# Low parts of weights on VectorE alone, splits drawn ahead and interleaved norms in a two-layer hybrid backbone

## The chip, the cores and the metric

The kernel runs on one core of a Trainium2 chip. The metric is the device time of one execution in microseconds (us). Four of the core's engines matter: TensorE (PE in the rows; PEld is its weight load), VectorE (DVE), ScalarE (ACT) and GpSimd (POOL). SyncE (SP) issues most DMA transfers. Every engine works through its own queue in order.

## What is computed

Two layers, an even one (Fourier mixing and a Hyena convolution) and an odd one (gated linear attention, GLA, and HGRN2), each with a feed-forward network (FFN) before and behind the mixer. There are 256 latent tokens and 256 context tokens, that is four tiles of 128 tokens; the context goes through the same weights with its own modulation. All is fp32. The part that this change touches is the FFN and its closing:

```python
def _modulate(x, shift, scale):
    return (_ln(x) * (1.0 + scale) + shift).astype(x.dtype)

def _post_ln(x, y, g, b):
    z = ALPHA * x.astype(jnp.float32) + y.astype(jnp.float32)
    return (_ln(z) * g + b).astype(x.dtype)

def _ffn_sublayer(x, shift, scale, gate, w_in, w_out, g, b):
    a, u = jnp.split(_modulate(x, shift, scale) @ w_in, 2, axis=-1)
    y = (jax.nn.silu(a) * u) @ w_out
    return _post_ln(x, 0.5 * gate * y, g, b)
```

D_MODEL is 1024 and D_FF is 2816, 22 blocks of 128. The modulation vectors (shift, scale, gate) are products of SiLU(c) and SiLU(c_ctx) with a weight of [1024, 9216] for each layer.

## The kernel before

**Weights.** An fp32 product is made of three products of a faster type: every weight unit `raw` [128, 1024] (512 KB, loaded on SP's queue into one of three buffers) is split into a high part `hi`, a cast on ACT (line 78), and a low part `lo = raw - hi` (line 79), on DVE or on POOL as the unit's flag `pool` says. Per block PE multiplies hi by hi, hi by lo and lo by hi (lines 463 to 465). `Stream.split_to(i)` emits the splits of all units up to i; `ahead_load` and `ahead_split` set how far loads and splits run ahead of use. Most split parts go into their own buffers (whi, wlo); units with the flag `spare` go into general buffers (S, names hi and lo).

**FFN, first product.** `ffn()` begins with a head of four units (`tm_head`), token tile by token tile; a head can only begin when the norm of its tile is there. Then 20 loops f = 2..21 have two units each (`pa` and `pu`, 24 matmuls of 512 columns each); behind them ACT makes SiLU(pa), DVE the product `sa` (line 617), and ACT and POOL split it into `hh` (lines 226 and 227). Between them `step(n)` advances background generators (`bg`) by n: mainly the modulation products, where each step multiplies one half of a weight block by both conditions, two DVE instructions `mt` (line 243), and, in one of the FFNs, the spectrum of the next mixer (tiles pr, eb).

**FFN, second product.** `ffn_close()` runs 22 units k over tiles 0 and 1 (pass 1, 12 matmuls for each k), then the same units over tiles 2 and 3 (pass 2). In pass 2 the last TAIL = 6 units run tile by tile: first tile 2, then tile 3, 36 matmuls each. `closing()` of a tile is post_ln (z, statistics st and mv, x), `norm` (mv, rstd, nb) and `to_hT`, the transposes that the next head needs. The closings of tiles 0 and 1 alternate in the background of pass 2; `done(t)` is called when a tile is ready, `fill(k)` behind each unit. Three FFNs of four tiles are closed thus, with keys c00, c01 and c10; the last FFN has two tiles and its own code.

**What sets the order.** The program is unrolled, and each engine takes its instructions in the order in which the Python code emits them; `bg`, `step`, `flush` and the table G, read through `g_(key, default)`, set it. The table's keys of the form c00l31 choose DVE (0) or POOL (1) for the low part of hT of a tile (here 3) and half (here 1).

Of the kernel before, what the change touches and what calls it, by code (L numbers as in the profile page):

```python
# [38 lines left out]
class Stream:  # L39
# [26 lines left out]
    def split_to(self, i):  # L66
        while self.n_split <= min(i, len(self.units) - 1):
# [3 lines left out]
            if split:  # L71
                w = self.raw.pop(j)
                if spare:
                    hi, lo = self.spare([P, 1024], F32R, "hi"), self.spare([P, 1024], F32R, "lo")
                else:
                    hi = self.pool.tile([P, 1024], F32R, tag="whi", name=f"whi{j}")
                    lo = self.pool.tile([P, 1024], F32R, tag="wlo", name=f"wlo{j}")
                self.nc.scalar.copy(hi, w)  # L78
                (self.nc.gpsimd if pool else self.nc.vector).tensor_tensor(lo, w, hi.bitcast(F32), op=ALU.subtract)  # L79
                self.split[j] = (hi, lo)  # L80
            self.n_split += 1

# [13 lines left out]


G0 = {"qlh33": 1, "qlh41": 1, "qlh43": 1, "of11": 2, "m0e00": 1, "qot12": 1, "m0l10": 0, "c10s2": 3, "c00S3": 2, "c10l30": 0, "m1w1": 1, "qot01": 0, "of": 2, "c10l31": 0, "o3": 4, "qoo0": 0, "m0l30": 0, "qeo6": 1, "c00l11": 0, "c00d2": 5, "qot23": 0, "ex21": 1, "es000": 1, "qei9": 1, "m0k": 0, "m0v2": 1, "fp3": 0, "ec010": 0, "ez3": 0, "fp1": 0, "qei3": 1, "m0l00": 0, "m0l01": 0, "qeo4": 0, "qeh2": 0, "ec012": 0, "es013": 0, "ec113": 0, "ec002": 1, "ec112": 0, "m0w0": 0, "m0v3": 1, "ec000": 1, "qei10": 1, "m0w1": 1, "m0a": -2, "m0v1": 1, "es003": 1, "m0w3": 1, "qei0": 0, "m0v0": 1, "m0l11": 1, "qeh0": 1, "es102": 1, "es012": 0, "qei2": 0, "m0e01": 1, "ez0": 1, "m0e10": 1, "qeh3": 1, "es100": 0, "m0e11": 1, "ex23": 1, "m0w2": 0, "es001": 1, "m0t3": 5, "c10w3": 1, "m0t2": 3, "qoi6": 1, "q00o14": 1, "o2": 1, "c00s2": 2, "qot02": 1, "m0d3": 2, "o1": 2, "m0s0": 2, "c01l01": 1, "of10": 1, "c00t3": 0, "c10w0": 0, "qoi16": 1, "c01l00": 1, "m0S1": 3, "m1w0": 1, "c00t1": 3, "qoi9": 1, "ex13": 1, "qoo6": 0, "m1l00": 1, "m1e11": 1, "of02": 3, "qoo7": 1, "c01d3": 3, "qoi14": 0, "m0t0": 2, "m1k": 6, "m1l10": 0, "qoi10": 0, "qoo5": 0, "of13": 3, "m0S2": 2, "m1e10": 0, "ec003": 0, "c10l10": 1, "qei8": 0, "of03": 4, "c00S2": 2, "qot20": 0, "c10e00": 0, "c00d3": 4, "m1a": 4, "of01": 3, "qot03": 0, "m0A": 2, "c01t3": 2, "q10o12": 1, "ec100": 0, "q01h0": 1, "qoi7": 0, "c10w1": 1, "qoi13": 0, "qot11": 0, "c00l10": 0, "m0s3": 2, "c00t2": 0, "c00l31": 1, "of12": 3, "c01d0": 3, "m1t0": 3, "qei4": 1, "qot32": 1, "c00F": 1, "c01S2": 2, "m1e01": 0, "qot00": 1, "m1l11": 0, "m1e00": 1, "c01v2": 1, "ok1": 2, "qlh02": 0, "c01l10": 0, "qoi15": 0, "SPN": 5, "qot21": 1, "q00o19": 0, "c00A": 2, "qoi11": 0, "qoi8": 1, "m1d0": 3, "c01S3": 2, "m0s1": 3, "m1d1": 5, "m1s1": 2, "ok0": 4, "of00": 1, "Fc0": 0, "Fw0": 1, "Ftl10": 1, "Ftl21": 1, "Fw2": 0, "Ftl11": 0, "Fc1": 1, "Ffl11": 0, "Fab0": 0, "Fte30": 0, "FxT11": 1, "Fs20": 0, "Ffl01": 0, "es101": 1, "qei5": 0, "m0e31": 1, "c01b2": 0, "m0e21": 0, "c10e21": 0, "qoo4": 0, "qlh00": 1, "qoo3": 0}
G = {}
SEEN = {}  # L100

# [27 lines left out]
def kernel(ctx: ExitStack, tc: tile.TileContext, a, out, stop=None):  # L129
# [450 lines left out]
    def queue_ffn(l, i):  # L580
# [4 lines left out]
                ws.add(a["ffn_in"][l, i, f, au], True, False, au == 1)  # L585
        for s in range(2):
            for k in range(KF):
                ws.add(a["ffn_out"][l, i, P * k:P * k + P, :], True, s == 1 and KF - TAIL <= k < KF - 1, g_(f"q{l}{i}o{k}", int(k % 2 == 1 and k < KF - 3)) if s and k > 11 else k % 2)

    def ffn(l, i, extra=(), head=None):  # L590
        hs = [{0: S([P, 2, 2, L], F32R, name="hh")} for s in range(2)]
# [9 lines left out]
        for f in range(2, KF):  # L601
# [9 lines left out]
                todo = None  # L611
            step(1)
            fm_unit(pu)
            step(2)
            sa = H([P, T], name="sa")
            act.activation(sa, pa, AF.Silu)
            dve.tensor_tensor(sa, sa, pu, op=ALU.mult)  # L617
# [5 lines left out]
    def ffn_close(l, i, hs, nxt):  # L623
# [9 lines left out]

        def fill(k):
            if k % 2:
                step(1)
            if k in range(10, 18, 2):
                next(loads)

        def closing(t, y, late=False):  # L640
            g, b, gates = ln
            return close(t, y, gates[t // 2], g, b, 2 * ALPHA, 4 * EPS, nxt, late, not late)

        y = tok_out(lhs, KF, (0, 1), fill)
        flush()
# [2 lines left out]
        bg.append(alternate(closing(0, y[0]), closing(1, y[1])))  # L648

        def done(t, y):  # L650
            if t == 3:
                hs.clear()
            ws.split_spare(ws.pos + g_(f"{k0}a{t}", 2 * t - 3))
            if t == 3:
                flush()
            bg.append(closing(t, y, True))
            now.append(t)

        def fill(k):
            if now:  # L660
                step(g_(f"{k0}s3", 1))
            elif k >= KF - TAIL:
                step(g_(f"{k0}s2", 1))
            else:
                if k >= KF - TAIL - 3:
                    ws.split_spare(ws.pos + g_(f"{k0}b{KF - TAIL - k}", 1))
                step(g_(f"{k0}s1", 2) if k > g_(f"{k0}s0", 2) else 1)

        now = []
        tok_out(lhs, KF, (2, 3), fill, TAIL, done)  # L670


# [55 lines left out]
    def spectrum(o, hd, w3, win, cs, skip, T=None):  # L728
# [78 lines left out]
        if early:  # L807
            for n in todo[:2]:
                pks[n] = product(*n)
                yield  # L810
        rs = scale()
        yield
# [1103 lines left out]
```

## Time and profile before

| quantity | value |
|---|---|
| median of 3 runs (lowest, highest) | 1894.14 us (1893.0, 1899.78) |
| profiled execution, time | 1893.39 us |
| its span | 1891.6 us |
| PE busy | 1761.0 us, 93% |
| DVE busy | 1259.5 us, 67% |
| ACT busy | 724.8 us, 38% |
| POOL busy | 721.6 us, 38% |

The rows of a later section are from this profiled execution. Times are counted from the start of its span. A row of a timeline gives the start, the duration, the engine, the line, the operation, what is written and read, and in brackets how long the engine had been idle before it and for what it had waited. PEclk is the granted clock of PE as a share of the full one.

### The profile page before, as it was taken

Reading aid. Unit: us, or ns where it says so; the run is one execution under the profiler, and the core shown is the slowest. Engines: PE = TensorE matmul, PEld = TensorE weight load, DVE = VectorE, ACT = ScalarE, POOL = GpSimd, SP = SyncE. Lnnn points to the kernel's source line nnn. Section 1 sums busy time; section 2 is a strip of 40 time slices with the busy share of each in tenths; the row PEclk is TensorE's granted clock in tenths of the full one; section 3 lists DMA queues with packets and bytes.
Section 4 is the critical chain, followed back from the end, with each engine's and each line's share of the span. In section 5 each row is a group of like instructions: output and inputs, shape, how many; then the busy total and the mean of one; then the engine's idle time right before and its main releaser. Section 6 shows DMA issues by size and latency. Waiting matters only on the chain. (4 is left out here: it accounts for less than half of the span.)

```text
span 1891.6 us, 22049 instructions
## 1 busy us (share of the span) xinstructions
PE 1761.0 (93%) x8236; PEld 1425.5 (75%) x8236; DVE 1259.5 (67%) x1674; ACT 724.8 (38%) x1070; POOL 721.6 (38%) x467
## 2 busy tenths in 40 slices
PE   6989999998987999999999999999988999879998
PEld 5767778876866778777887787788867778757887
DVE  6688887267599768885247688812377484676755
ACT  5422233344434342223334422323354463443443
POOL 2445434453356223333445233334454353341000
PEclk9989999999998999999999999999999999889999
DMA  8536654644313145553464455433644223335563
GB/s 317 214 132 240 227 189 166 238 167 150 112 45 123 65 164 202 208 203 130 154 233 177 150 213 199 162 110 138 232 166 145 83 91 90 134 131 201 206 215 137
DMA packets 91499, 314.91 MB, mean 166 GB/s; under 512 B 10848, under 2 KB 11584, under 8 KB 91392
## 3 DMA queue, kind: packets, MB, share of 16 engines
q1 hardware_dynamic: 85952, 297.09, 44.0%
q0 software_dynamic: 4576, 15.91, 2.6%
q8 instruction: 64, 1.05, 0.2%
q10 hardware_dynamic: 864, 0.51, 0.1%
q14 instruction: 43, 0.35, 0.1%
HBM read 308.18 MB, written 4.24 MB: 165 GB/s over the span
## 5 line engine op out<-in xcount | busy, mean ns | idle before, releaser
L79 DVE TENSOR_TENSOR wlo<-raw,whi 128x1024 fp32r<-128x1024 f32 x195 | 261.5, 1343 | 330.7 <-ACT whi L78 328.9
L79 POOL TENSOR_TENSOR wlo<-raw,whi 128x1024 fp32r<-128x1024 f32 x137 | 345.9, 2525 | 316.9 <-ACT whi L78 278.4
L78 ACT CAST whi<-raw 128x1024 fp32r<-128x1024 f32 x332 | 343.8, 1050 | 264.9 <-PE y L465 151.9
L243 DVE SCALAR_TENSOR_TENSOR mt<-mraw,cb 128x1024 bf16<-128x1024 f32 x256 | 395.8, 1599 | 11.2 <-DMA mraw<-in_mod_w_dram 8.3
L465 PE MATMUL pu<-hT,wlo 128*128 128x512 f32 x576 | 225.7, 392 | 4.7 <-DVE wlo L79 4.7
L463 PE MATMUL pu<-hT,whi 128*128 128x512 f32 x576 | 225.8, 392 | 0.0
L464 PE MATMUL pu<-hT,whi 128*128 128x512 f32 x576 | 225.4, 391 | 0.0
L227 POOL TENSOR_TENSOR hh<-sa,hh 128x256 fp32r<-128x256 f32 x120 | 87.1, 747 | 344.6 <-ACT hh L226 344.6
L465 PE MATMUL pa<-hT,wlo 128*128 128x512 f32 x480 | 191.3, 398 | 12.0 <-DVE wlo L79 12.0
L463 PE MATMUL pa<-hT,whi 128*128 128x512 f32 x480 | 191.5, 399 | 8.8 <-ACT whi L78 8.7
L464 PE MATMUL y<-wlo,hh 128*128 128x512 f32 x468 | 183.2, 391 | 6.8 <-DVE wlo L79 6.1
L464 PE MATMUL pa<-hT,whi 128*128 128x512 f32 x480 | 189.1, 394 | 0.0
L463 PE MATMUL y<-whi,hh 128*128 128x512 f32 x468 | 182.9, 391 | 0.2 <-ACT whi L78 0.2
L465 PE MATMUL y<-whi,hh 128*128 128x512 f32 x468 | 182.2, 389 | 0.0
L226 ACT CAST hh<-sa 128x256 fp32r<-128x256 f32 x120 | 42.8, 404 | 294.7 <-DVE sa L617 294.7
L465 PEld LDWEIGHTS pu<-hT,wlo 128*128 128x128 f32 x576 | 108.8, 189 | 28.3 <-DVE wlo L79 5.6
L463 PEld LDWEIGHTS pu<-hT,whi 128*128 128x128 f32 x576 | 109.0, 189 | 23.6 <-ACT hh L226 0.8
L464 PEld LDWEIGHTS pu<-hT,whi 128*128 128x128 f32 x576 | 108.9, 189 | 22.6
L465 PEld LDWEIGHTS pa<-hT,wlo 128*128 128x128 f32 x480 | 91.3, 190 | 39.7 <-DVE wlo L79 21.1
L463 PEld LDWEIGHTS pa<-hT,whi 128*128 128x128 f32 x480 | 91.4, 190 | 34.3 <-ACT whi L78 15.7
L464 PEld LDWEIGHTS y<-wlo,hh 128*128 128x128 f32 x468 | 87.8, 188 | 28.6 <-DVE wlo L79 8.4
L464 PEld LDWEIGHTS pa<-hT,whi 128*128 128x128 f32 x480 | 91.4, 190 | 18.7
(419 smaller groups left out, 3272.2 us busy)
## 6 DMA issues: line engine op xcount, KB each, us to landing
raw<-in_ffn_out_dram SPq DMA_DIRECT2D x154, 512.0 KB, 3.4
mraw<-in_mod_w_dram SPq DMA_DIRECT2D x144, 512.0 KB, 5.9
raw<-in_ffn_in_dram SPq DMA_DIRECT2D x120, 512.0 KB, 3.8
raw<-in_ffn_tm_dram SPq DMA_DIRECT2D x44, 512.0 KB, 3.3
raw<-in_od_fm_dram SPq DMA_DIRECT2D x17, 512.0 KB, 3.2
raw<-in_od_tm_dram SPq DMA_DIRECT2D x16, 512.0 KB, 3.3
raw<-in_ffn_head_dram SPq DMA_DIRECT2D x12, 512.0 KB, 4.4
raw<-in_ev_in_dram SPq DMA_DIRECT2D x12, 512.0 KB, 3.5
```

The lines of the kernel that those rows point to most:

```text
L78: self.nc.scalar.copy(hi, w)
L79: (self.nc.gpsimd if pool else self.nc.vector).tensor_tensor(lo, w, hi.bitcast(F32), op=ALU.subtract)
L226: act.copy(dst_hi, src)
L227: (lo_eng or dve).tensor_tensor(dst_lo, src, dst_hi.bitcast(F32), op=ALU.subtract)
L243: dve.scalar_tensor_tensor(H([P, D], BF16, "mt"), w, 1.0, cb[s], op0=ALU.mult, op1=ALU.mult, accum_out=acc[:, s, b:b + 1])
L463: pe.matmul(o, lhsT=wh, rhs=xh, start=start, stop=False)
L464: pe.matmul(o, lhsT=wh, rhs=xl, start=False, stop=False)
L465: pe.matmul(o, lhsT=wl, rhs=xh, start=False, stop=stop)
```

## The change

- Every low part of a weight is made on DVE; the flags `pool` no longer have an effect. 164 lows move from POOL to DVE.
- Four more low parts of hT (tile 3) go to DVE.
- In pass 2 the units k = 13 to 20 use general buffers for their split parts, before only 16 to 20; the buffers of hh are released unit by unit (`pop`) and not at the end.
- The loops of the first product take 1 and 2 background steps in turn behind `pu`, before always 2.
- In pass 2 `split_to` runs ahead by up to four units more from k = 11 on, and during tile 2's tail it splits the next head's four units. `done(2)` no longer splits; `done(3)` interleaves the closings of tiles 2 and 3 in the order 2, 3, 2, 3, 3, 2.
- A spectrum that is not early waits three empty steps before its scaling.

```diff
-                (self.nc.gpsimd if pool else self.nc.vector).tensor_tensor(lo, w, hi.bitcast(F32), op=ALU.subtract)
+                self.nc.vector.tensor_tensor(lo, w, hi.bitcast(F32), op=ALU.subtract)
...
+G0.update({f"{k}l3{g}": 0 for k in ("c00", "c01", "c10", "m0") for g in range(2)})
...
-                ws.add(a["ffn_out"][l, i, P * k:P * k + P, :], True, s == 1 and KF - TAIL <= k < KF - 1, ...
+                ws.add(a["ffn_out"][l, i, P * k:P * k + P, :], True, s == 1 and KF - TAIL - 3 <= k < KF - 1, ...
...
-            step(2)
+            step(1 + f % 2)
...
         def fill(k):
             if k % 2:
+                hs[0].pop(k // 2)
                 step(1)
...
         def done(t, y):
-            if t == 3:
+            if t == 2:
+                flush()
+                ln[2][0] = None
+                bg.append(closing(t, y, True))
+                older.append(bg[-1])
+            else:
                 hs.clear()
-            ws.split_spare(ws.pos + g_(f"{k0}a{t}", 2 * t - 3))
-            if t == 3:
-                flush()
-            bg.append(closing(t, y, True))
+                g2, g3 = older.pop(), closing(t, y, True, True)
+                for g in (g2, g3, g2, g3, g3, g2):
+                    next(g, None)
+                bg.clear()
+                bg.extend([g2, g3])
             now.append(t)
 
         def fill(k):
             if now:
-                step(g_(f"{k0}s3", 1))
+                step(1)
             elif k >= KF - TAIL:
-                step(g_(f"{k0}s2", 1))
+                step(1)
+                ws.split_to(first + min(KF + k - (KF - TAIL), KF + 3))
             else:
-                if k >= KF - TAIL - 3:
-                    ws.split_spare(ws.pos + g_(f"{k0}b{KF - TAIL - k}", 1))
+                if k % 2:
+                    hs[1].pop(k // 2)
                 step(g_(f"{k0}s1", 2) if k > g_(f"{k0}s0", 2) else 1)
+                ws.split_to(first + k + 2 + {11: 1, 12: 1, 13: 2, 14: 3, 15: 4}.get(k, 0))
...
+        else:
+            for _ in range(3):
                 yield
         rs = scale()
```

The first place is a loop of the first product of the second FFN, on DVE: wlo is the low part of a weight unit, mt a modulation product, sa the product behind the two units. Before:

```order
L79 TENSOR_TENSOR wlo_6638<-raw_6546,whi_6637 128x1024
L243 SCALAR_TENSOR_TENSOR mt_6667,acc_6530<-mraw_6612,cb_5443 128x1024
L243 SCALAR_TENSOR_TENSOR mt_6669,acc_6530<-mraw_6612,cb_5445 128x1024
L243 SCALAR_TENSOR_TENSOR mt_6703,acc_6530<-mraw_6618,cb_5443 128x1024
L243 SCALAR_TENSOR_TENSOR mt_6705,acc_6530<-mraw_6618,cb_5445 128x1024
L243 SCALAR_TENSOR_TENSOR mt_6707,acc_6530<-mraw_6665,cb_5443 128x1024
L243 SCALAR_TENSOR_TENSOR mt_6709,acc_6530<-mraw_6665,cb_5445 128x1024
L617 TENSOR_TENSOR sa_6711<-sa_6711,pu_6634 128x512
```

One low part and six mt stand between two products. The same engine and place in the changed kernel:

```order
L79 TENSOR_TENSOR wlo_6599<-raw_6507,whi_6598 128x1024
L244 SCALAR_TENSOR_TENSOR mt_6628,acc_6408<-mraw_6573,cb_5443 128x1024
L244 SCALAR_TENSOR_TENSOR mt_6630,acc_6408<-mraw_6573,cb_5445 128x1024
L79 TENSOR_TENSOR wlo_6635<-raw_6543,whi_6634 128x1024
L244 SCALAR_TENSOR_TENSOR mt_6664,acc_6408<-mraw_6579,cb_5443 128x1024
L244 SCALAR_TENSOR_TENSOR mt_6666,acc_6408<-mraw_6579,cb_5445 128x1024
L618 TENSOR_TENSOR sa_6668<-sa_6668,pu_6595 128x512
```

A second low part, from POOL, stands between the mt, and this loop has four mt; the next one has six.

The second place is the end of tile 2 in pass 2 of the first FFN, on DVE. raw86 and raw87 are the last two units of the pass, raw88 to raw91 the next head's; z is the sum at the start of tile 2's closing. Before:

```order
L79 TENSOR_TENSOR lo459_3443<-raw86_3416,hi458_3442 128x1024
L79 TENSOR_TENSOR wlo87_3455<-raw87_3428,whi87_3454 128x1024
L331 TENSOR_TENSOR z464_3494<-y414_3013,gate413_2921 128x512
L337 SCALAR_TENSOR_TENSOR z464_3494<-x30_175,z464_3494 128x512
L338 BN_STATS st465_3495<-z464_3494 128x6
```

The closing follows the pass's last low part at once. In the changed kernel:

```order
L79 TENSOR_TENSOR wlo87_3437<-raw87_3410,whi87_3436 128x1024
L79 TENSOR_TENSOR lo467_3449<-raw88_3428,hi466_3448 128x1024
L79 TENSOR_TENSOR lo469_3461<-raw89_3434,hi468_3460 128x1024
L79 TENSOR_TENSOR lo471_3473<-raw90_3446,hi470_3472 128x1024
L79 TENSOR_TENSOR lo473_3485<-raw91_3458,hi472_3484 128x1024
L332 TENSOR_TENSOR z474_3506<-y414_3013,gate413_2921 128x512
```

The four lows of the next head now stand ahead of the closing.

The third place is between the closings of tiles 2 and 3, on DVE: x, st and mv, rp and nb are the end of tile 2's, the second z is tile 3's. Before:

```order
L353 SCALAR_TENSOR_TENSOR x469_3526<-z464_3494,rstd467_3516,lnb411_2845 128x1024
L304 BN_STATS st472_3543<-x469_3526 128x6 x2
L306 BN_AGGR mv473_3546<-st472_3543 128x2
L79 TENSOR_TENSOR lo475_3551<-raw90_3464,hi474_3550 128x1024
L233 TENSOR_SCALAR rp479_3561<-mv473_3546 128x1
L395 SCALAR_TENSOR_TENSOR nb471_3542<-mv473_3546,rstd478_3560 128x1
L331 TENSOR_TENSOR z485_3582<-y416_3015,gate413_2921 128x512
```

A low part of the head stood within tile 2's norm, and tile 3 began behind it. In the changed kernel:

```order
L354 SCALAR_TENSOR_TENSOR x479_3538<-z474_3506,rstd477_3528,lnb411_2844 128x1024
L305 BN_STATS st482_3555<-x479_3538 128x6 x2
L307 BN_AGGR mv483_3558<-st482_3555 128x2
L234 TENSOR_SCALAR rp485_3561<-mv483_3558 128x1
L332 TENSOR_TENSOR z486_3564<-y416_3015,gate413_2921 128x512
L396 SCALAR_TENSOR_TENSOR nb481_3554<-mv483_3558,rstd484_3560 128x1
L338 SCALAR_TENSOR_TENSOR z486_3564<-x41_221,z486_3564 128x512
```

Tile 3's first instruction stands between rp and nb of tile 2, and the low part is gone from here.

## Rows read from the trace of the kernel before

**Rows 1.** Windows by stage: us, busy time (and instructions) by engine, PEclk, DMA share, GB/s.

```profile
95.00:319.00 224.00, 206.23 (x895) 164.62 (x894) 190.35 (x235) 58.03 (x94) 95.02 (x65) 0.96 0.53 192
319.00:381.00 62.00, 62.00 (x275) 51.33 (x274) 15.84 (x13) 26.31 (x28) 33.37 (x20) 1.00 0.66 228
381.00:441.00 60.00, 55.54 (x244) 43.62 (x243) 43.33 (x52) 29.51 (x37) 31.26 (x16) 1.00 0.51 176
480.00:648.00 168.00, 151.43 (x702) 123.68 (x701) 141.39 (x203) 67.69 (x106) 78.51 (x45) 0.95 0.26 90
687.00:916.00 229.00, 222.68 (x970) 180.25 (x969) 164.37 (x207) 65.31 (x105) 79.79 (x60) 1.00 0.51 189
1074.00:1289.00 215.00, 210.77 (x923) 171.77 (x922) 137.67 (x172) 63.09 (x100) 73.57 (x57) 1.00 0.49 177
1421.00:1459.00 38.00, 30.77 (x199) 28.32 (x197) 28.64 (x38) 19.24 (x35) 15.10 (x10) 0.91 0.37 129
```

The engines stand in the order PE, PEld, DVE, ACT, POOL.

**Rows 2.** Waits of PE over the span: waiting <- releaser: us, stops, mean us.

```profile
PE pa L465 <- DVE wlo L79: 12.0, 21, 0.6
...
PE pa L463 <- ACT whi L78: 8.7, 13, 1.7
...
PE pr L758 <- DVE eb L803: 7.6, 1, 7.6
```

**Rows 3.** The page's costliest groups: busy us, mean ns | idle before, releaser.

```profile
L79 DVE TENSOR_TENSOR wlo<-raw,whi 128x1024 fp32r<-128x1024 f32 x195 | 261.5, 1343 | 330.7 <-ACT whi L78 328.9
L79 POOL TENSOR_TENSOR wlo<-raw,whi 128x1024 fp32r<-128x1024 f32 x137 | 345.9, 2525 | 316.9 <-ACT whi L78 278.4
...
L243 DVE SCALAR_TENSOR_TENSOR mt<-mraw,cb 128x1024 bf16<-128x1024 f32 x256 | 395.8, 1599 | 11.2 <-DMA mraw<-in_mod_w_dram 8.3
L465 PE MATMUL pu<-hT,wlo 128*128 128x512 f32 x576 | 225.7, 392 | 4.7 <-DVE wlo L79 4.7
```

**Rows 4.** Timeline of a loop of the second FFN, ACT, DVE and POOL.

```profile
843.76 2.00 ACT L78 CAST whi<-raw 128x1024 fp32r<-128x1024 f32 x2
...
845.89 2.51 POOL L79 TENSOR_TENSOR wlo<-raw,whi 128x1024 fp32r<-128x1024 f32 x1 [0.82 <-POOL hh L227]
846.07 3.41 DVE L243 SCALAR_TENSOR_TENSOR mt<-mraw,cb 128x1024 bf16<-128x1024 f32 x1
849.41 1.21 DVE L243 SCALAR_TENSOR_TENSOR mt<-mraw,cb 128x1024 bf16<-128x1024 f32 x1
...
855.14 0.68 DVE L617 TENSOR_TENSOR sa<-sa,pu 128x512 f32<-128x512 f32 x1
856.34 1.43 POOL L227 TENSOR_TENSOR hh<-sa,hh 128x256 fp32r<-128x256 f32 x2 [7.94 <-ACT hh L226]
856.48 2.00 ACT L78 CAST whi<-raw 128x1024 fp32r<-128x1024 f32 x2
857.55 1.30 DVE L79 TENSOR_TENSOR wlo<-raw,whi 128x1024 fp32r<-128x1024 f32 x1 [1.73 <-ACT whi L78]
```

**Rows 5.** Timeline of DVE, closings of tiles 2 and 3 of the first FFN.

```profile
441.09 0.69 DVE L331 TENSOR_TENSOR z<-y,gate 128x512 f32<-128x512 f32 x1 [0.82 <-PE y L465]
...
449.13 3.41 DVE L353 SCALAR_TENSOR_TENSOR x<-z,rstd,lnb 128x1024 f32<-128x1024 f32 x1 [0.44 <-POOL rstd L234]
...
456.01 0.68 DVE L331 TENSOR_TENSOR z<-y,gate 128x512 f32<-128x512 f32 x1
...
468.39 0.16 DVE L395 SCALAR_TENSOR_TENSOR nb<-mv,rstd 128x1 f32<-128x1 f32 x1 [0.73 <-POOL rstd L234]
```

**Rows 6.** DMA issues in 400:450: count, KB each, median us to landing.

```profile
raw<-in_ffn_out_dram SPq DMA_DIRECT2D x11, 512.0 KB, 3.3
raw<-in_ev_tm_dram SPq DMA_DIRECT2D x4, 512.0 KB, 4.3
```

**Rows 7.** Timeline of DVE at the end of the odd mixer, two OG scalings.

```profile
1641.88 1.14 DVE L1419 SCALAR_TENSOR_TENSOR OG<-OG,rr,rg 128x128 f32<-128x128 f32 x4 [1.12 <-POOL rr L234]
...
1652.59 5.41 DVE L1419 SCALAR_TENSOR_TENSOR OG<-OG,rr,rg 128x128 f32<-128x128 f32 x4 [1.16 <-POOL rr L234]
```

More of the change, by code (lines that the diff above doesn't have):

```diff
@@ L587, in queue_ffn @@
             for k in range(KF):
-                ws.add(a["ffn_out"][l, i, P * k:P * k + P, :], True, s == 1 and KF - TAIL <= k < KF - 1, g_(f"q{l}{i}o{k}", int(k % 2 == 1 and k < KF - 3)) if s and k > 11 else k % 2)
+                ws.add(a["ffn_out"][l, i, P * k:P * k + P, :], True, s == 1 and KF - TAIL - 3 <= k < KF - 1, g_(f"q{l}{i}o{k}", int(k % 2 == 1 and k < KF - 3)) if s and k > 11 else k % 2)
     def ffn(l, i, extra=(), head=None):
@@ L638, in fill, with closing @@
                 next(loads)
-        def closing(t, y, late=False):
+        def closing(t, y, late=False, fine=False):
             g, b, gates = ln
-            return close(t, y, gates[t // 2], g, b, 2 * ALPHA, 4 * EPS, nxt, late, not late)
+            return close(t, y, gates[t // 2], g, b, 2 * ALPHA, 4 * EPS, nxt, late, fine or not late)
         y = tok_out(lhs, KF, (0, 1), fill)
@@ L660, in fill @@
             if now:
-                step(g_(f"{k0}s3", 1))
+                step(1)
             elif k >= KF - TAIL:
-                step(g_(f"{k0}s2", 1))
-            else:
-                if k >= KF - TAIL - 3:
-                    ws.split_spare(ws.pos + g_(f"{k0}b{KF - TAIL - k}", 1))
+                step(1)
+                ws.split_to(first + min(KF + k - (KF - TAIL), KF + 3))
+            else:
+                if k % 2:
+                    hs[1].pop(k // 2)
                 step(g_(f"{k0}s1", 2) if k > g_(f"{k0}s0", 2) else 1)
-        now = []
+                ws.split_to(first + k + 2 + {11: 1, 12: 1, 13: 2, 14: 3, 15: 4}.get(k, 0))
+        now, older = [], []
+        first = ws.pos
         tok_out(lhs, KF, (2, 3), fill, TAIL, done)
@@ L809, in spectrum @@
                 pks[n] = product(*n)
+                yield
+        else:
+            for _ in range(3):
                 yield
```

## The prediction, made before the result was known

> **What bounds the kernel now.** I read the busy line first: TensorE (PE) is busy 1761.0 of 1891.6 us, so at most some 130 us can be won, and what is looked for is where PE stands idle and who ends that. The windows by stage come next [rows 1]. In the three stages that run the first products of the four-tile FFNs (95:319, 687:916, 1074:1289), PE lacks 224.00−206.23 = 17.8, 229.00−222.68 = 6.3 and 215.00−210.77 = 4.2 us, 28.3 together. The granted clock was 0.96 in the first, which is another 0.04×224 = 9.0. The waits of PE over the whole span say who ends this [rows 2]: 12.0 us of pa behind the low part wlo on VectorE (DVE), 8.7 behind the cast whi on ScalarE (ACT), 7.6 behind one eb tile of the spectrum; 28.3 again. Those are 35 stops, and each also breaks the pipelining: a matmul is on the page with .39 us (225.7/576) [rows 3] where one every 62.00/275 = .2255 is the rate of the stage in which PE never stops [rows 1]; 35×.16 = 5.6. So these loops hold 28.3+9.0+5.6 = 43 us.
>
> Why they wait is seen in one loop of the second FFN [rows 4]. The pair of casts starts at 843.76 and again at 856.48: 12.7 us a loop, in which PE has 48 matmuls, 48×.2255 = 10.8 us. DVE is the long leg: its first mt takes 3.41 where the next takes 1.21, and the 3.41 is the one that runs while GpSimd (POOL) makes the other low part (845.89, 2.51 us). Over the kernel the 256 mt average 1599 ns [rows 3], (1.60−1.21)×256 = 100 us more than alone, and the 195 lows on DVE average 1343, against the same 1.21 for an op of that size 26 us more. So POOL's 137 lows, 2.5 us each, cost DVE 126 us, .9 each. A low that moves costs DVE 1.21, frees about .9, and is there 1.3 us sooner.
>
> **FFN loops (the lo line and step(1+f%2)).** DVE's leg of a loop afterwards, by [rows 4]: from the product's end (855.14+.68 = 855.82) to the next low 1.73; two lows and four or six mt, mean five, at 1.14 each (1.21, less .07 by which the mt of 846.07 still ran when the next began); the product .68. That is 9.3 or 11.5, mean 10.4, under PE's 10.8. The casts and hh steps are unchanged. So the 43 us go, but for a residual: a loop with six mt is .7 over PE, and ten of them in the first FFN, where mod steps fill all loops, give 7 if nothing buffers them; I take 6 there and 1 in each of the others: 8. The three empty yields of the spectrum are there for the 7.6 wait, which I count as gone: if they do not reach it, it stays. **−35**, bounds −43 and −18: the upper end if the lows keep 1.34 and an mt 1.3, which makes 1.73+2×1.27+5×1.23+.68 = 11.1, .3×60 loops = 17 lost.
>
> Fewer mod steps in the loops (50 instead of 60 an FFN) push the rest of the first FFN's mods into pass 1, at most seven pairs, 7×2×1.21 = 17 us; DVE is busy 15.8 of 62 there and PE 62.00 [rows 1], so PE hides them, unless they delay the eleven lows that come over from POOL there.
>
> The Trainium skill has a rule that speaks against this term: "SBUF — State Buffer", "Who interferes with whom", says that a DVE instruction with two SBUF inputs contends with a GpSimd instruction that reads SBUF, and that issue order decides who blocks. The rows above bear it out for the lows. The hh lows stay on POOL, and by the rule they could block DVE too; what that would make is the third rival below.
>
> **Closings and next heads (split_to in pass 2, done, the G0 entries, spare buffers, earlier pops).** Three FFNs have this. Take the first, with T = 441.09, where tile 2's matmuls have ended and its z starts [rows 5]. Tile 3's z starts at 456.01 = T+14.9, its nb at 468.39 = T+27.3. One op between them, x at 449.13, takes 3.41 where one of its kind and size takes 1.21 alone [rows 4]. Afterwards the four lows of the next head stand on DVE ahead of tile 2's z. When can the last be there? A unit needs a raw buffer of three for landing, cast 1.0 [rows 4] and low 1.2: with the landings in [rows 6], (3.3+2.2)/3 = 1.8 us a unit of the second product, (4.3+2.2)/3 = 2.2 of the head. The table asks for nine units in five k's, 5×12×.2255 = 13.5 us, while the buffers give them in 9×1.8 = 16.5: 3 late; the head's four need 8.8 where tile 2's tail lasts 36×.2255 = 8.1. So the last head low comes about T+4, and with landings of 4.3 throughout T+7. The closing's DVE work behind it is 14.9 less 2.2 (x) and 1.2 (a head low, now ahead), 11.5; then tile 3's, which is interleaved from here, some 12.4 as before: nb of tile 3 at T+28 to T+31, against T+27.3. The pass itself ends about 1.3 sooner, by a low's gain, unless DVE is short: 43.3 busy in 381:441, plus twelve lows at 1.21 less .9, 3.7, is 47 of 60. I take +1 in each of the three, **+3**, bounds −5 (T comes sooner and the lows are in time) and +7 (landings 4.3, and PE stands for the head) in each. The G0 entries move four hT lows; spare buffers for three more units and the pops only free memory sooner, hidden as long as PE has units in hand; their cost is within these bounds.
>
> By the Trainium skill, "DMA: Bandwidth & Descriptors", "Anatomy of one DMA — SWDGE (gpsimd) path", 512 KB take an estimated 2.0+524288/436e3 = 3.2 us. The trace has 3.3 for one stream and 4.3 for the head's, on SP's queue rather than GpSimd's [rows 6]. By the page's figure the head's lows would come 4×1.1/3 = 1.5 sooner, 4.5 us less in all, 1850; the sum keeps the rows' 4.3.
>
> **The odd mixer's end.** One scaling, OG at 1652.59, takes 5.41 against 1.14 [rows 7], 4.3 us, behind POOL lows. Three lows move there, 3×1.21 = 3.6 on DVE. **−3**, bounds −4.3 and +1.
>
> **Elsewhere.** Some 32 more lows move in the first head, the two mixers, the heads and the last FFN. In the even mixer (480:648) eight do, DVE is busy 141.4 of 168 and PE idle 16.6 [rows 1]; by the .9 above DVE gets 8×.3 = 2.4 more work and the lows come sooner. I take a fourth of PE's idle time there and nothing in the rest: **−4.5**, bounds −9 and +8.
>
> **Sum.** −35+3−3−4.5 = −39.5, made against the profiled execution's 1893.39: 1853.9. The median of the runs shown is .75 higher: 1854.6, forecast **1855**. Its own range, with FFN loops from −43 to −18 and the small bounds partly together, is 1841 to 1872.
>
> **Rivals.** *DVE becomes the bound of the second passes.* There DVE's in-order queue mixes lows with closings that wait. If its busy share stays at today's 43.33/60 = .72, the 47 us take 65 where PE needs 59: 6 late, three times, 18 instead of the 3: 1870. For it: lows that wait for casts block closings behind them. Against it: DVE reaches .85 (190.35/224) in the FFN loops and needs 47/59 = .80 here, where it is level.
>
> *Early heads pay in full.* If the lows are in by T, the closing of tile 2 comes 2.2+1.2 = 3.4 sooner and T itself 1.3, three times, 14 instead of the +3: 1838. PE's idle time and lost clock behind T bound it: 7.2+.09×38 = 10.7 in 1421:1459, the longest of the three [rows 1]. Against it: the buffer count above.
>
> *POOL's hh lows now block DVE.* Two of them a loop, 1.43 for the pair [rows 4]; if DVE stood still for them, its leg is 10.4+1.5 = 11.9, 1.1 over PE where today it is 1.9 over: 43×1.1/1.9 = 25 of the 43 stay, 1893.4−18−4.5 = 1871, 1872 as median. Against it: they run at 856.34 to 857.77, while DVE waits for the cast, and the low at 857.55 takes 1.30 instead of 1.21.
>
> *Slower: the stalls are not POOL's.* Suppose the long mt come from something that stays, the traffic of the landing loads. The loop's leg is then 1.73+2×1.34+5×1.60+.68 = 13.1, against 12.7: 2.3 over PE, 43×2.3/1.9 = 52, 9 more than now. In the second passes DVE has 43.3+12×1.34 = 59.4, at its .85 70 us where PE needs 60: 10 late, three times, 30. With nothing won elsewhere 1893.4+9+30 = 1932. It decides from the point at which the loop is as long as now, a mean mt of (12.7−1.73−2×1.34−.68)/5 = 1.5. Against it: the next mt of the same loop, with loads under way alike, takes 1.21. That the change does not do what it says, and leaves the stalls, is this case.
>
> **Chances.** Forecast .60; DVE the bound of the passes .18; hh lows .07; early heads .10; slower .05. Each rival carries the small bounds about it. 1837 to 1880 leaves out the slower case, nearly half of the early heads' and two ninths of the passes': .05+.045+.04, and .04 of the forecast's own edges. About 0.5%, 9.5 us, is what a measurement can tell here; 1884.7 and above is reached by the late end of the passes' case (.04, the same) and by the slower one (.05): faster .91, same .04, slower .05.
>
> **What would show it.** DVE busy about 1259+164×1.21−126−25 = 1306, the 25 for other stalled ops; mt mean under 1.3 and DVE lows near 1.21; POOL's low line gone. PE's idle time in the three FFN stages at most 10 together, no 7.6 wait of pr. Tile 2's z 4 to 7 us behind its last matmul, and tile 3's z ahead of tile 2's nb. If mt stay at 1.6, the main step is wrong; if PE waits for wlo with mt at 1.2, the loop's leg is mis-sized; if PE stands in the second passes for lows, the passes' case holds.

## The result, and the profile after

| | before | changed |
|---|---|---|
| median of 4 runs (lowest, highest) | 1895.55 us (1893.0, 1899.78) | 1831.41 us (1828.71, 1833.63) |
| profiled execution, span | 1891.6 us | 1828.6 us |
| PE busy | 1761.0 us | 1738.7 us |
| DVE busy | 1259.5 us | 1275.8 us |
| POOL busy | 721.6 us | 304.3 us |

The ratio is 0.9659 with an interval of 0.9635 to 0.9682, 60 to 69 us less. The forecast was 1855 with a range from 1837 to 1880: the direction was right, and the gain was 24 us larger than forecast and lies outside the range.

The page of the changed kernel, busy line and costliest groups (busy us, mean ns, idle time before them); the low parts of units with the flag spare have a row of their own here:

```profile
PE 1738.7 (95%) x8236; PEld 1419.6 (78%) x8236; DVE 1275.8 (70%) x1841; ACT 725.5 (40%) x1070; POOL 304.3 (17%) x300
...
L79 DVE TENSOR_TENSOR wlo<-raw,whi 128x1024 fp32r<-128x1024 f32 x323 | 410.3, 1274 | 303.1 <-ACT whi L78 302.6
...
L244 DVE SCALAR_TENSOR_TENSOR mt<-mraw,cb 128x1024 bf16<-128x1024 f32 x256 | 309.8, 1251 | 2.0 <-DMA mraw<-in_mod_w_dram 2.0
...
L79 DVE TENSOR_TENSOR lo<-raw,hi 128x1024 fp32r<-128x1024 f32 x72 | 92.6, 1295 | 50.9 <-ACT hi L78 50.4
```

Against [rows 3] the mean mt went from 1599 to 1251 ns and the POOL row of 345.9 us is gone. DVE took over 167 instructions (POOL's fall from 467 to 300): the 164 lows of weights and three low parts of hT, not four, whose row on POOL goes from 19 to 16. DVE is only 16 us busier.

The stages were cut at PE's own marks: the last matmul of a head, the first of a second product, the first of the odd mixer's input and of its token-major part (tm). The times between them, in us:

| stage | before | changed | lows alone | steps alone | lows back on POOL |
|---|---|---|---|---|---|
| start to first loops | 66.6 | 66.6 | 66.4 | 69.1 | 67.7 |
| loops, first FFN | 254.8 | 226.1 | 236.9 | 235.2 | 235.5 |
| its second product, closing, even mixer, next head | 363.7 | 366.7 | 367.3 | 373.2 | 368.7 |
| loops, second FFN | 229.7 | 218.8 | 218.8 | 219.6 | 219.6 |
| its second product, closing, next head | 158.4 | 160.2 | 158.7 | 158.2 | 161.2 |
| loops, third FFN | 224.8 | 218.3 | 218.2 | 218.3 | 218.2 |
| its second product, closing | 131.3 | 127.4 | 127.4 | 131.1 | 129.7 |
| odd mixer to tm | 94.2 | 95.4 | 92.5 | 93.0 | 94.2 |
| tm to the last FFN's loops | 188.9 | 173.5 | 180.0 | 190.8 | 190.6 |
| last FFN | 171.1 | 167.6 | 167.9 | 171.1 | 171.6 |

From before to changed the loops give 28.7+10.9+6.5 = 46.1, the odd mixer 14.2, the last FFN 3.5; the three stretches with closings take 3.0+1.8−3.9 = 0.9 more. Together 62.9 of the span's 63.0. Each column is one profiled execution; those of the last three columns are the slowest of their four, 3.6, 2.1 and 1.9 us over the median.

### The profile page after: what moved, and what is told of

It reads as the page before. It is cut to its first block, busy times and chain, and to the rows that moved or that the text cites. A ratio compares the mean times of both kernels' runs of the same rounds, so it can differ in the third digit from the quotient of the medians.

```text
span 1828.6 us, 22049 instructions
## 1 busy us (share of the span) xinstructions
PE 1738.7 (95%) x8236; PEld 1419.6 (78%) x8236; DVE 1275.8 (70%) x1841; ACT 725.5 (40%) x1070; POOL 304.3 (17%) x300
## 5 line engine op out<-in xcount | busy, mean ns | idle before, releaser
L79 DVE TENSOR_TENSOR wlo<-raw,whi 128x1024 fp32r<-128x1024 f32 x323 | 410.3, 1274 | 303.1 <-ACT whi L78 302.6
L78 ACT CAST whi<-raw 128x1024 fp32r<-128x1024 f32 x323 | 337.7, 1052 | 336.1 <-PE y L466 122.0
L244 DVE SCALAR_TENSOR_TENSOR mt<-mraw,cb 128x1024 bf16<-128x1024 f32 x256 | 309.8, 1251 | 2.0 <-DMA mraw<-in_mod_w_dram 2.0
L464 PE MATMUL pa<-hT,whi 128*128 128x512 f32 x480 | 187.6, 391 | 0.0
L466 PE MATMUL pa<-hT,wlo 128*128 128x512 f32 x480 | 186.8, 389 | 0.0
L465 PE MATMUL pa<-hT,whi 128*128 128x512 f32 x480 | 186.7, 389 | 0.0
L465 PE MATMUL y<-wlo,hh 128*128 128x512 f32 x432 | 169.0, 391 | 3.6 <-DVE wlo L79 3.6
L464 PE MATMUL y<-whi,hh 128*128 128x512 f32 x432 | 168.7, 390 | 0.0
L466 PE MATMUL y<-whi,hh 128*128 128x512 f32 x432 | 168.3, 389 | 0.0
L79 DVE TENSOR_TENSOR lo<-raw,hi 128x1024 fp32r<-128x1024 f32 x72 | 92.6, 1295 | 50.9 <-ACT hi L78 50.4
L235 POOL TENSOR_TENSOR rstd<-rp,mhalf 128x1 f32<-128x1 f32 x42 | 36.3, 868 | 490.2 <-DVE rp L234 487.2
```

The source lines that it names most:

```text
L79: self.nc.vector.tensor_tensor(lo, w, hi.bitcast(F32), op=ALU.subtract)
L235: gp.tensor_tensor(dst, t, mhalf.to_broadcast([P, n]), op=ALU.pow)
L244: dve.scalar_tensor_tensor(H([P, D], BF16, "mt"), w, 1.0, cb[s], op0=ALU.mult, op1=ALU.mult, accum_out=acc[:, s, b:b + 1])
L464: pe.matmul(o, lhsT=wh, rhs=xh, start=start, stop=False)
L465: pe.matmul(o, lhsT=wh, rhs=xl, start=False, stop=False)
L466: pe.matmul(o, lhsT=wl, rhs=xh, start=False, stop=stop)
```

## The experiments

Each run was compared with runs of the kernel before on the same chip; ratios are to those, and the changed kernel has 0.9659.

**The lows alone.** Edit on the kernel before:

```diff
-                (self.nc.gpsimd if pool else self.nc.vector).tensor_tensor(lo, w, ...
+                self.nc.vector.tensor_tensor(lo, w, ...
```

> The kernel before with one edit: every low part of a weight on DVE. Theory P (POOL's lows hold DVE up): a loop's leg on DVE is 1.73+2x1.14+6x1.14+.68 = 11.5 us, .7 over PE's 10.8 where it was 1.9 over, so some 16 of the loops' 45 us stay and 29 go; the odd mixer's 13 go whole, the last FFN and its head give 5: about 1848 us, 47 under before, mt near 1.25 on average. Rival S (the fewer steps and the empty yields carry the loops): the loops gain under 15 and the total is over 1865. Rival C (the rewritten closing carries a good part): second passes and heads come out worse than before by 5 or more each, total over 1860.

1840.64 us, ratio 0.9707 (0.9686 to 0.9728): 55 us of the 64, 8 more than expected. The expected order of sizes holds, with more from the loops (35 instead of 29) and less from the mixer than "whole". Neither rival's condition is met.

**The steps alone.**

```diff
-            step(2)
+            step(1 + f % 2)
```

> The kernel before with one edit: 1 and 2 steps in turn behind pu instead of 2. Theory P: the stalled mt stays, the leg is 12.7-1.14 = 11.5 on average, so the loops can gain up to 43x1.2/1.9 = 27, but one mt a loop still takes 3.4 and the rest of the mods falls into pass 1 beside POOL's lows: 10 to 20 less in the loops, nothing in the odd mixer, total 1875 to 1885. Rival S: 35 or more less, total under 1862.

1867.26 us, ratio 0.9846 (0.9827 to 0.9865). This missed the expectation: the loops give 36.2 us, as much as with the lows alone, though every low stays where it was. That meets the first half of rival S (35 or more in the loops), but not the second (under 1862). The stretch behind the first loops takes 9.5 back, 4 of them in the second product (from its start to tile 2's tail 113.1 us instead of 109.0), into which the rest of the mods falls. PE, DVE and granted clock in the loops of the three FFNs, by windows (us; busy time and instructions of PE, PEld, DVE, ACT, POOL; PEclk, DMA share, GB/s), first of before, then of the lows alone, the steps alone and the changed kernel:

```profile
66.60:321.40 254.80, 237.03 (x1028) 188.48 (x1027) 209.67 (x259) 71.46 (x114) 109.99 (x77) 0.97 0.54 196
685.10:914.80 229.70, 222.43 (x969) 179.81 (x968) 164.92 (x209) 65.22 (x104) 80.35 (x62) 1.00 0.51 189
1073.20:1298.00 224.80, 220.57 (x965) 179.89 (x964) 138.98 (x173) 65.82 (x103) 76.99 (x59) 1.00 0.48 174
```

```profile
66.40:303.40 237.00, 230.04 (x1029) 186.00 (x1029) 196.70 (x280) 71.61 (x114) 55.29 (x54) 0.99 0.58 210
670.70:889.50 218.80, 218.80 (x969) 180.72 (x968) 153.28 (x227) 66.82 (x104) 28.36 (x40) 1.00 0.53 195
1048.10:1266.40 218.30, 218.30 (x966) 180.61 (x965) 136.05 (x193) 66.90 (x103) 27.85 (x39) 1.00 0.49 178
```

```profile
69.10:304.30 235.20, 229.79 (x1029) 185.77 (x1028) 192.81 (x227) 70.83 (x113) 114.19 (x77) 0.99 0.56 201
677.50:897.00 219.50, 218.78 (x968) 180.69 (x967) 170.70 (x209) 66.15 (x104) 85.25 (x61) 1.00 0.55 197
1055.30:1273.50 218.20, 218.20 (x965) 180.56 (x964) 143.28 (x173) 66.34 (x103) 82.61 (x59) 1.00 0.51 179
```

```profile
66.60:292.60 226.00, 226.00 (x1028) 185.21 (x1027) 181.42 (x252) 71.77 (x114) 55.98 (x54) 1.00 0.58 208
659.30:878.10 218.80, 218.80 (x968) 180.69 (x967) 154.75 (x227) 65.82 (x104) 28.36 (x40) 1.00 0.55 195
1038.30:1256.60 218.30, 218.30 (x966) 180.61 (x965) 137.34 (x193) 66.35 (x103) 27.84 (x39) 1.00 0.49 176
```

In the second and third FFN either edit by itself lets PE run through, or all but .7 us. In the first each leaves some 10 us, and only both together make PE's busy time equal to the window. Loops of the run with the steps alone, on DVE, show why:

```profile
790.40 0.68 DVE L617 TENSOR_TENSOR sa<-sa,pu 128x512 f32<-128x512 f32 x1
792.81 1.30 DVE L79 TENSOR_TENSOR wlo<-raw,whi 128x1024 fp32r<-128x1024 f32 x1 [1.74 <-ACT whi L78]
...
795.17 3.40 DVE L243 SCALAR_TENSOR_TENSOR mt<-mraw,cb 128x1024 bf16<-128x1024 f32 x1
...
800.80 0.68 DVE L617 TENSOR_TENSOR sa<-sa,pu 128x512 f32<-128x512 f32 x1
...
834.42 0.68 DVE L617 TENSOR_TENSOR sa<-sa,pu 128x512 f32<-128x512 f32 x1
```

The stalled mt is there as before, but with four mt the loop is 800.80−790.40 = 10.4 long. A loop with six mt still takes before's 12.7, but only one loop in four has them: loops have two and three steps in turn, and about every second one with three spends a step on the sum that ends a modulation vector (line 247), which is no mt. So four loops in a row take 834.42−790.40 = 44.0 us, 11.0 each. With the lows alone, and in the kernel before, loops of six, six and four mt follow one another. Three such loops of the second FFN, from product to product, first with the lows alone, then before:

```profile
781.62 0.68 DVE L617 TENSOR_TENSOR sa<-sa,pu 128x512 f32<-128x512 f32 x1
...
814.32 0.68 DVE L617 TENSOR_TENSOR sa<-sa,pu 128x512 f32<-128x512 f32 x1
```

```profile
806.41 0.68 DVE L617 TENSOR_TENSOR sa<-sa,pu 128x512 f32<-128x512 f32 x1
...
842.42 0.68 DVE L617 TENSOR_TENSOR sa<-sa,pu 128x512 f32<-128x512 f32 x1
```

That is 32.7/3 = 10.9 and 36.0/3 = 12.0 us a loop, where PE itself needs 218.80/20 = 10.9. Either edit takes the mean leg from 1.1 over PE to within .1 of it, and the stage times agree, 218.8 and 219.6, 218.2 and 218.3: what decides is the mean length of DVE's leg and not which edit shortens it. Both expectations missed this, since they took 11.5 for the mean leg.

The first FFN is not this leg alone, though 236.9 and 235.2 are near one another too. About half of PE's idle time there, 7.0 us with the lows alone and 5.4 with the steps alone, is one wait for the spectrum (us, times, longest; in this order):

```profile
PE pr L758 <- DVE eb L803: 4.0, 1, 4.0
```

```profile
PE pr L758 <- DVE eb L803: 2.5, 1, 2.5
```

**The closing as it was.** The changed kernel with the second product's fill and done functions and the spare flags of before.

```diff
-                ws.split_to(first + min(KF + k - (KF - TAIL), KF + 3))
...
+            ws.split_spare(ws.pos + g_(f"{k0}a{t}", 2 * t - 3))
+            if t == 3:
+                flush()
+            bg.append(closing(t, y, True))
```

> The changed kernel with the closing of the FFNs as it was (no splits drawn ahead, no interleaving, spare buffers and hh released as before), lows all on DVE, steps and yields as changed. By the stage ledger the three closings with their heads cost -0.1 us net between the two kernels, so theory P has 1826 to 1837, the same as the changed kernel. Rival C: the closing was worth 10 or more beside the DVE lows, 1841 or more.

1830.49 us, ratio 0.965 (0.9633 to 0.9667): the same as the changed kernel. The rewritten closing, the early splits and the released buffers bring nothing measurable in total. In this run's trace the three stretches with closings take 651.3 us instead of the changed kernel's 654.3, and the stretch from tm to the last loops 177.9 instead of 173.5.

**The lows back on POOL.** The changed kernel with the first edit undone.

> The changed kernel with the lows back on POOL where the flags had them; steps, yields, early splits and interleaving as changed. If the two ways of relieving the loops (lows, steps) stand in for one another, the second and third FFN keep their gain (10 and 6.5 us) and the first loses about 9 of its 28.8, as in the run with the steps alone; the odd mixer loses its 14 and the last FFN its 3.6; the early head lows, 2.4 us each on POOL, hold the closings up. Theory P: 1865 to 1880. If the new closing works only with the lows on DVE, 1880 or more; if it has a gain of its own that the DVE lows hid, under 1860.

1865.03 us, ratio 0.9821 (0.9799 to 0.9844), at the lower edge of the 1865 to 1880 expected. By the table it is the steps alone again, and the mixer's and the last FFN's gains are gone (190.6 and 171.6). That POOL's lows of the head hold the closings up does not show in their sum: the three stretches take 659.6 us, with the steps alone 662.5.

**Three lows of the odd mixer, twice.** Both edits are on the kernel before. First the three of the rc block:

```diff
-                ws.add(a["od_tm"][n, kp], True, n == 3, g_(f"qot{n}{kp}", kp % 2))
+                ws.add(a["od_tm"][n, kp], True, n == 3, 0 if n == 3 else g_(f"qot{n}{kp}", kp % 2))
```

> The kernel before with three lows of the odd mixer moved to DVE, those of the last block of its token-major weights (rc), two of which stood on POOL beside the eight OH scalings that took 6.44 us in the trace of before and 2.18 in that of after. If that one stall and the clock that falls behind it carry the odd mixer's gain, 8 to 12 of its 14 us go, PE's stop for am (4.4 us) shortens to about 1.9, and the total is 1884 to 1888. If the gain is spread over all of the odd mixer's 18 lows, or comes from the lows as such, at most 4: 1891 to 1895.

1897.05 us, ratio 1.0 (0.9987 to 1.0013): nothing. The edit had missed its aim, since the two lows beside the OH scalings were others. So the three of the output weights:

```diff
-            ws.add(a["od_out"][P * k:P * k + P, :], True, k < 5, g_(f"qoo{k}", int(k < 5)))
+            ws.add(a["od_out"][P * k:P * k + P, :], True, k < 5, 0)
```

> The kernel before with three lows of the odd mixer's output weights moved to DVE; the run with the three rc lows left the OH scalings at 6.4 us, so that the pair of lows on POOL beside them (616.76 behind 1000, 4.83 us) must be of the output weights. If the stall of the OH scalings is what the odd mixer loses, they take 2.2 instead of 6.4 here, PE's stop for am falls from 4.4 to about 2, and from tm to the last FFN's loops the kernel takes 178 to 181 us instead of 188.9: total 1885 to 1889. If the lows matter as such, wherever they stand, as little as the other three: 1893 to 1898.

1885.5 us, ratio 0.9938 (0.9918 to 0.9958), within the range of the first expectation. From tm to the last loops it takes 176.1 us instead of 188.9. The rows, timelines of DVE and POOL, are first of the rc run, then of the run with the output weights' lows:

```profile
1619.66 6.43 DVE L1419 SCALAR_TENSOR_TENSOR OH<-OH,rr,gn 128x128 f32<-128x128 f32 x8
...
1620.59 4.83 POOL L79 TENSOR_TENSOR lo<-raw,hi 128x1024 fp32r<-128x1024 f32 x2
```

```profile
1616.98 2.18 DVE L1419 SCALAR_TENSOR_TENSOR OH<-OH,rr,gn 128x128 f32<-128x128 f32 x8
```

The eight scalings fall from 6.43 to 2.18 us, and the waits of PE (us, times, longest) say who had been behind them. Of before and of the changed kernel:

```profile
PE po L1351 <- DVE am L1345: 4.4, 1, 4.4
PE y L464 <- DVE wlo L79: 1.9, 1, 1.9
```

```profile
PE po L1365 <- DVE am L1359: 1.8, 1, 1.8
```

The run with the output weights' lows has no such wait for am. It doesn't have the stop of 1.9 us for a low either, so that its gain is not all of the OH scalings. Six lows were moved in these two runs; three gave 11.5 us and three gave nothing. It is not the low as such that costs, but what stands beside it and who waits for that.

**The three empty steps.** The changed kernel without them.

```diff
-        else:
-            for _ in range(3):
-                yield
         rs = scale()
```

> The changed kernel without the three empty steps of the spectrum. PE waited 7.6 us for eb once in the kernel before, 4.0 in the run with the lows alone, and not at all in the run with the steps alone, which has no empty steps either. By that the fewer steps have removed the wait and the empty ones do nothing: within 4 us of the changed kernel, no wait of pr over 1 us. If they are what removed it: 4 to 8 slower, 1835 to 1840, with the wait of pr back.

1829.34 us, ratio 0.9642 (0.9626 to 0.9659), and no wait of pr at all. They do nothing here. Of the premises in that expectation one was wrong: with the steps alone pr did wait, 2.5 us (before 7.6, lows alone 4.0).

**The even mixer's lows on POOL.** The changed kernel with eight lows, units 92 to 115, by their flags.

```diff
-                self.nc.vector.tensor_tensor(lo, w, ...
+                (self.nc.gpsimd if pool and 92 <= j < 116 else self.nc.vector).tensor_tensor(lo, w, ...
```

> The changed kernel with the eight lows of the even mixer and the head behind it back on POOL. From the start of the first pass 1 to the loops of the second FFN the changed kernel takes 366.7 us and the kernel before 363.7. If the eight lows on a busy DVE cost those 3 us (PE's wait for z, 2.64 before, 4.98 after), it is 2 to 5 faster than the changed kernel: 1826 to 1830. If POOL's lows stall DVE there as elsewhere, 2 to 8 slower: 1833 to 1840.

1826.43 us, ratio 0.9621 (0.9605 to 0.9638), 5 less than the changed kernel, with intervals that just touch. In the profiled executions the spans differ by 1.9 us (1826.7 and 1828.6), of which the stage has 1.1 (365.6 instead of 366.7), and the changed kernel's four executions lie 4.9 us apart. So it is not shown that this edit gains anything.

**The head's lows in the closing.** Two edits on the changed kernel, each alone: the last two head lows behind the start of tile 2's closing, and the head's raw units outside the ring of three.

```diff
             if now:
                 step(1)
+                ws.split_to(first + min(KF + 2 + k - (KF - TAIL), KF + 3))
             elif k >= KF - TAIL:
                 step(1)
-                ws.split_to(first + min(KF + k - (KF - TAIL), KF + 3))
+                ws.split_to(first + min(KF + k - (KF - TAIL), KF + 1))
```

```diff
-            if self.bufs is None:
+            if self.bufs is None or j in (88, 89, 90, 91, 200, 201, 202, 203, 288, 289, 290, 291):
```

> The changed kernel, with the last two of the next head's four lows drawn in during tile 3's tail, behind the start of tile 2's closing, instead of ahead of it. In the changed kernel z of tile 2 starts at 420.87, 8 us behind its last matmul, right behind the last head low. If that order holds the closing up, z starts 3 to 5 us sooner, nb of both tiles too, and PE's wait of 8 us for xn at the head shortens: 4 us each, total 1818 to 1824. If the loads set the time of the head (raw buffers), or the head then waits for its lows, the total is 1829 to 1836 with the wait at another place.

> The changed kernel with the four raw units of the next head in general buffers instead of the ring of three, at each of the three closings; the order of all instructions is the same. In the changed kernel each cast of these units waits for its load and tile 2's z stands 7.6 us behind the last matmul of tile 2. If the ring of three sets that time, the loads start sooner, z comes 3 to 6 us sooner and the total is 1818 to 1827. If the transfers themselves do (SP's order, the queues), z stays within 1.5 us and the total within 1829 to 1834.

1824.7 us, ratio 0.9619 (0.9586 to 0.9652), and 1823.88 us, 0.9616 (0.9595 to 0.9636). Timelines of the first closing, ACT's casts and DVE, first of the changed kernel, then with the general buffers:

```profile
413.98 1.05 ACT L78 CAST hi<-raw 128x1024 fp32r<-128x1024 f32 x1 [1.05 <-DMA raw<-in_ev_tm_dram]
417.27 1.05 ACT L78 CAST hi<-raw 128x1024 fp32r<-128x1024 f32 x1 [2.24 <-DMA raw<-in_ev_tm_dram]
418.64 1.05 ACT L78 CAST hi<-raw 128x1024 fp32r<-128x1024 f32 x1 [0.32 <-DMA raw<-in_ev_tm_dram]
...
418.36 2.60 DVE L79 TENSOR_TENSOR lo<-raw,hi 128x1024 fp32r<-128x1024 f32 x2 [2.07 <-ACT hi L78]
420.87 0.68 DVE L332 TENSOR_TENSOR z<-y,gate 128x512 f32<-128x512 f32 x1
...
430.08 0.68 DVE L332 TENSOR_TENSOR z<-y,gate 128x512 f32<-128x512 f32 x1
430.89 0.16 DVE L396 SCALAR_TENSOR_TENSOR nb<-mv,rstd 128x1 f32<-128x1 f32 x1
...
442.08 0.16 DVE L396 SCALAR_TENSOR_TENSOR nb<-mv,rstd 128x1 f32<-128x1 f32 x1
```

```profile
415.07 1.05 ACT L78 CAST hi<-raw 128x1024 fp32r<-128x1024 f32 x1 [0.23 <-DMA raw<-in_ev_tm_dram]
416.35 1.05 ACT L78 CAST hi<-raw 128x1024 fp32r<-128x1024 f32 x1 [0.22 <-DMA raw<-in_ev_tm_dram]
...
413.59 5.07 DVE L79 TENSOR_TENSOR lo<-raw,hi 128x1024 fp32r<-128x1024 f32 x4 [0.19 <-ACT hi L78]
418.57 0.68 DVE L332 TENSOR_TENSOR z<-y,gate 128x512 f32<-128x512 f32 x1
```

In the changed kernel each cast waits for its load and z comes right behind the fourth low. Pass 2's last matmul starts at 421.06, so tile 2's ends at about T = 421.06−36×.2255+.2 = 413.1: z is at T+7.8. With general buffers the four lows run without a gap and z is at T+3.9; with two lows later it is at T+3.3. The stretch of the second closing shrinks from 160.2 to 155.8 and 157.3. So the ring of three does set the time of the head's lows, and they set the closing. The gain is not the 4 us at each closing that was hoped for: the first stretch has 2 us less with either edit, the third (127.1 and 127.0 instead of 127.4) next to nothing. In total each is worth some 7 us, at the edge of what the intervals can tell.

**Combined.** First the later lows with the even mixer's lows on POOL, then all three edits.

> Two edits on the changed kernel that each gave time alone: two of the head's lows later (6.7 us) and the eight lows of the even mixer on POOL (5.0). They lie in different stages, except that the even mixer follows the first closing: if they add up, 1831.4-11.7 = 1820, between 1817 and 1823. If the second one only shortened what the first one shortens too, 1824 to 1827.

> The changed kernel with three edits that each gave 5 to 7 us alone: two of the head's lows later, the even mixer's lows on POOL, the head's raw units in general buffers. The first two together gave 5.8, not 11.7. In the trace of the run with general buffers tile 2's z still waits for the fourth head low (T+3.9), and in the run with later lows for the second (T+3.3): the two reach for the same 4 us at each closing. If that is all they have, 1820 to 1825; if the later lows can use the sooner loads, z at T and tile 3's closing 3 us sooner, 1812 to 1818.

1825.58 us, ratio 0.9624 (0.9607 to 0.9641): they do not add up, and beside the later lows (1824.7) the even mixer's lows on POOL bring nothing. With all three 1818.19 us (1814.02 to 1819.41, 5 runs), ratio 0.9582 (0.9568 to 0.9596), between the two expectations and next to the lower one. This interval is clear of the changed kernel's: 1818 is the fastest version measured, 13 us below it by the medians. In its trace z of tile 2 has moved ahead of two of the four lows.

## Why the prediction was outside its range

**The cause of the stalls was right.** The rival that ended slower, stalls that are not POOL's, is refuted by the run with the lows alone: mt falls from 1599 to 1254 ns on its page.

```profile
L243 DVE SCALAR_TENSOR_TENSOR mt<-mraw,cb 128x1024 bf16<-128x1024 f32 x256 | 309.5, 1254 | 2.3 <-DMA mraw<-in_mod_w_dram 2.3
```

POOL's hh lows, the third rival, do not take their place: in the changed kernel mt is at 1251 and PE does not wait in the loops. The price of .9 us a low was a little high: it divides by the 137 lows of one row, where 164 ran on POOL; nothing hangs on it.

**The loops' term was mis-sized: −35 forecast, −46.1 measured.** The step that failed is the length of DVE's leg. The prediction took the loop of [rows 4], 12.7 us, for the mean one, and for afterwards four and six mt in turn, ten loops of six in the first FFN. Counted on DVE, before has loops of six, six and four (12.0 on average in the second FFN, 1.1 over PE and not 1.9), and the changed kernel mostly of six, four, four and four: of 19 loops from product to product in the first FFN five have six mt, and the mean is 4.3. By the prediction's own sum that makes 1.73+2×1.14+4.3×1.14+.68 = 9.6 instead of 10.4, and the residual of 8 falls away. The loop of six is over PE by itself, as predicted, here 770.55−758.54 = 12.0, but the next one, with four, takes 9.8, and PE does not stop:

```profile
758.54 0.69 DVE L618 TENSOR_TENSOR sa<-sa,pu 128x512 f32<-128x512 f32 x1 [0.75 <-issue]
...
770.55 0.68 DVE L618 TENSOR_TENSOR sa<-sa,pu 128x512 f32<-128x512 f32 x1
...
780.30 0.69 DVE L618 TENSOR_TENSOR sa<-sa,pu 128x512 f32<-128x512 f32 x1 [0.31 <-issue]
```

PE's busy time is 226.00 of 226.00 in the first FFN, 218.80 of 218.80 and 218.30 of 218.30 in the others. The base of 43 was also 3 short: over the whole loops PE's idle time before was 29.3 us instead of the 28.3 in the windows of [rows 1], and its busy time fell by 16.9, where the prediction had 9.0 for the clock and 5.6 for the stops. So the lower bound of −43 was the value to expect, not an end. The rivals' scaling, 43 us for 1.9 over PE, went by the same loop of 12.7; no run here has a mean leg between 11.0 and 12.0 in the second FFN, so how the loss grows between them is not shown.

**The odd mixer's term was mis-sized: −3 forecast, −14.2 measured.** The prediction read one long scaling, OG [rows 7], and not the eight OH scalings before it, which stood beside two lows on POOL and which PE's stop for am waited for. In the trace of before:

```profile
1615.83 6.44 DVE L1419 SCALAR_TENSOR_TENSOR OH<-OH,rr,gn 128x128 f32<-128x128 f32 x8
...
1616.76 4.83 POOL L79 TENSOR_TENSOR lo<-raw,hi 128x1024 fp32r<-128x1024 f32 x2
```

The granted clock is the other half of it. Windows of this stretch, from before, the changed kernel, the lows alone, the closing as it was and the run with the output weights' lows:

```profile
1608.00:1676.00 68.00, 58.95 (x315) 47.86 (x314) 43.52 (x69) 24.95 (x41) 22.84 (x15) 0.87 0.34 124
```

```profile
1562.00:1620.00 58.00, 53.20 (x317) 43.25 (x315) 39.81 (x77) 26.29 (x42) 8.48 (x9) 0.97 0.43 144
```

```profile
1569.00:1633.00 64.00, 59.34 (x317) 48.41 (x315) 39.81 (x76) 26.18 (x42) 8.49 (x9) 0.87 0.40 131
```

```profile
1555.00:1617.00 62.00, 57.79 (x316) 47.26 (x315) 39.48 (x76) 25.70 (x42) 8.48 (x9) 0.89 0.40 134
```

```profile
1608.00:1666.00 58.00, 55.25 (x328) 44.90 (x326) 40.58 (x73) 26.15 (x42) 16.32 (x13) 0.97 0.45 148
```

Half clock costs .13×68 = 8.8 us there before and .03×58 = 1.7 after, 7 of the 14. Of the rest 2.6 us are the stop for am and 1.9 the stop for a low, which is gone. The prediction's sum charged the clock in the loops alone. With the lows alone the scalings are short too (2.18) but the clock stays at .87, and the stage from tm on is 180.0 instead of 173.5: .13×64 is 8.3 instead of 1.7, the whole difference. So short scalings alone do not keep the clock up: the lows alone and the closing as it was have them at .87 and .89, the run with the output weights' lows and the changed kernel at .97. That these scalings were stalled by POOL and what the stall costs is shown; why the clock falls there in some of these runs is open.

**The closings' sum came near the forecast, in part by luck.** +1 was forecast for each; the three stretches took 3.0 (even mixer included) and 1.8 more and 3.9 less. The third's gain comes with the lows and not with the new closing: it takes 127.4 us with the lows alone and 127.7 with the closing as it was, against 131.3 before. The early lows were put at T+4 to T+7 and z came behind them at T+7.8; tile 3's nb was put at T+28 to T+31 and came at T+29.0. The count of raw buffers was the right limit, and the run with general buffers shows it in the first closing. That DVE becomes the bound of the second passes did not happen; nor did the early heads pay in full.

**Elsewhere**, −4.5 was forecast; the last FFN gave 3.5, the start nothing, the even mixer none of the fourth of its idle time that was hoped for. That stretch became 3 longer, in the run with the lows alone too. The spectrum's wait of 7.6 is gone as counted on, but not by the empty steps.

In sum the loops gave 11 more, the odd mixer 11 more, the closings with the even mixer 2 more and the rest 1 less: 23 of the 24 us between 1855 and 1831.

## What to carry to other kernels

- Where two engines hold each other up, don't price the moved instruction but list the long instructions beside it: of six lows in the odd mixer three were worth 11.5 us and three nothing.
- Take the leg of a loop as the mean over several loops, and count how often each kind comes: with splits ahead, single loops of 12.0 us did not stop an engine that needs 10.9, while the mean was no longer. Two edits that each bring the mean down to the bound engine's are substitutes, and their gains must not be added.
- Before moving loads' consumers ahead, count the buffers that the loads land in: the early splits waited for a ring of three, and held up the closing that stood behind them.

## What the runs showed of the hardware

A low on POOL blocks even a small DVE instruction for its whole length. The eight OH scalings of the run with the rc lows, by tile (count, then shortest, median and longest in ns, first and last start):

```profile
L1419 DVE SCALAR_TENSOR_TENSOR OH<-OH,rr,gn x8: 337/346/2473, 1619.7 to 1625.8; 128x128 f32<-128x128 f32 x8
```

The median is 346 ns, and the longest has the 2.4 us of a POOL low (4.83 for two). The Trainium skill ("SBUF — State Buffer", "Who interferes with whom") says that a DVE instruction with two SBUF inputs contends with a GpSimd instruction that reads SBUF, and that the port pair they share is an exclusive lock; the trace agrees. By the same rule the hh lows left on POOL, .7 us each, could block DVE too; no run shows a loss by them.

The granted clock in the odd mixer's stretch was 0.87 in the run with the lows alone, 0.89 with the closing as it was and 0.97 in the changed kernel, although PE's stops for am there are nearly the same, 2.1, 1.6 and 1.8 us. What the engine did otherwise before it fell was not settled.
